# Newton's step of the norms in three instructions on VectorE, and two output transfers on ScalarE's queue

## The chip, the cores and the metric

The kernel runs on one core of a Trainium2 chip. The core has a matrix engine (TensorE, PE in the profile, with its weight loads as PEld), a vector engine (VectorE, DVE), a scalar engine (ScalarE, ACT), a general one (GpSimd, POOL) and SyncE (SP), which here only issues transfers. Each engine takes the instructions of its own queue in order. The metric is device time in microseconds (us); lower is better.

## The reference

Two layers of a hybrid block work on 512 latent tokens and 256 context tokens of width 1024. Layer 0 mixes by convolutions, layer 1 by windowed attention; each layer ends with a ConvFFN of inner width 2816, and the latents get a last RMSNorm. Every norm needs one inverse root per token:

```python
def rmsnorm(x, g):
    xf = x.astype(jnp.float32)
    y = xf * lax.rsqrt(jnp.mean(xf * xf, axis=-1, keepdims=True) + EPS)
    return (y * g.astype(jnp.float32)).astype(x.dtype)

x = x + g1 * y                                   # mixer of the layer
x = x + g2 * conv_ffn(modulate(rmsnorm(x, norm_ffn[l]), sh2, sc2), w_up[l], w_conv_ffn[l], w_down[l])
...
return rmsnorm(x, final_norm)
```

The layer norm in the convolution mixer uses the same inverse root.

## The kernel before

The activations lie transposed: 128 features on the partitions, tokens along the free axis, eight tiles `x[k]` of 128 features. A matrix product with a weight tile is made of three products of split operands (lines 185 to 187: low part of the weights, low part of the activations, both high parts). Weights come in by SyncE's queue (line 172), ScalarE casts the high part (line 166) and VectorE subtracts the low part (line 167).

A norm goes so. While the last product of a sub-layer is closed column by column (`project`, with `gate_in` at line 372 and `square_in` at lines 291 to 296), the squares are added up in `ss`. TensorE turns `ss` into one sum per token (line 303, the statistics), ScalarE adds the epsilon (line 306, tile `rv`), and `inverse` makes the inverse root `y`: a first guess on the bits (line 308) and three Newton steps of four instructions each (lines 310 to 313), on two, four or six numbers per partition. `rstd` spreads `y` on the diagonal of a tile `rd` (line 325, VectorE) and TensorE broadcasts it over the partitions (line 335); ScalarE copies the result to `r` (lines 444, 540, 646), and `mod_in` makes the next `h` from it (line 348 on VectorE, lines 357 to 362 on ScalarE and VectorE), which the next products read (lines 220 to 224, `side_by_side`).

`inverse` is used eleven times. The norm at the start and the two at the end pass VectorE as the engine. The other eight go through `rstd` with its default, GpSimd: two in the layer norm of the convolutions (`conv_norm`), and one for each of two token segments at the first ConvFFN, at the start of layer 1 and at the second ConvFFN (`spread`, called by `tokens_in_turn`). In `tokens_in_turn` the first segment's norm is made while TensorE still has columns of the second segment to do: `project` holds columns back (`late`), and lines 328 to 331 ask that two or three of them stand between the statistics and the broadcast.

The order in which the instructions of each engine stand in its queue is made when the kernel is built, by a planner that works with estimated durations (`schedule_with_timeline_sim=True`, line 1249). `issue_after` adds an edge to that order; it isn't a wait at run time.

At the end, `final` scales the transposed results by `y` into eight tiles `fo` of 128x512 and sends each out by a transfer of 256 KB (line 1156), all on SyncE's queue. The last four tiles (`both=True`) are made in turn by ScalarE (line 1154) and VectorE (line 1152).

Of the kernel before, what the change touches and what calls it, by code (L numbers as in the profile page):

```python
# [17 lines left out]
ALU = mybir.AluOpType  # L18
PSUM = bass.MemoryType.PSUM

P = 128
# [43 lines left out]
class Kern:  # L65
# [232 lines left out]
    def inverse(self, ss, chunks, ones2, comp, eng):  # L298

        nc = self.nc  # L300
        n = len(chunks)
        for i, c in enumerate(chunks):
            self.stats = nc.tensor.matmul(comp[:, 2 * i:2 * i + 2], ss[:, c:c + P], ones2, start=True, stop=True)
        v, y, t = (self.tmp.tile([P, 6], F32, name=g, tag=g)[:, :n] for g in ("rv", "ry", "rt"))
        means = comp[:, :2 * n].rearrange("p (n c) -> p n c", c=2)[:, :, 0:1].squeeze(2)
        self.means = nc.scalar.activation(v, means, AF.Copy, bias=EPS)

        eng.tensor_scalar(y.bitcast(I32), v.bitcast(I32), -0.5, float(0x5F3759DF), op0=ALU.mult, op1=ALU.add)
        for _ in range(3):
            eng.tensor_tensor(t, y, y, op=ALU.mult)  # L310
            eng.tensor_tensor(t, t, v, op=ALU.mult)
            eng.tensor_scalar(t, t, -0.5, 1.5, op0=ALU.mult, op1=ALU.add)
            eng.tensor_tensor(y, t, y, op=ALU.mult)
        return y

    def rstd(self, ss, segs, ones2, slot, eng=None, pool=None, project=None):

        nc = self.nc
        chunks = [c for lo, hi in segs for c in range(lo, hi, P)]
        n = len(chunks)  # L320
        o = slot
        off = segs[0][0] - segs[0][0] % C0
        y = self.inverse(ss, chunks, ones2, o[:, segs[0][0] - off:segs[0][0] - off + 2 * n], eng or nc.gpsimd)
        d = (pool or self.tmp).tile([P, n, P], F32, name="rd", tag="rd", bufs=1)
        nc.vector.tensor_tensor(
            d, self.ident.unsqueeze(1).broadcast_to([P, n, P]), y.unsqueeze(2).broadcast_to([P, n, P]), op=ALU.mult
        )
        if project:
            with self.tc.issue_after(self.stats.ins):
                next(project)  # L330
        i = 0
        with self.tc.issue_after(self.product.ins) if project else nullcontext():
            for lo, hi in segs:
                m = (hi - lo) // P
                nc.tensor.matmul(
                    o[:, lo - off:hi - off], self.onesm, d[:, i:i + m, :].rearrange("p n c -> p (n c)"), start=True, stop=True)
                i += m
        return o[:, segs[0][0] - off:segs[-1][1] - off]
# [805 lines left out]
    def final(self, seg, slots, y, both=True):  # L1144

        nc = self.nc
        for i, s in enumerate(slots):
            half, c = divmod(i, 2)
            tag, bufs = (("tC", 2), ("tC", 2), ("r", 1), ("rd", 1))[i] if both else (("tA", "tB")[c], 2)
            o = self.tmp.tile([P, 512], F32, name="fo", tag=tag, bufs=bufs)  # L1150
            if both and c:
                nc.vector.tensor_scalar(o, s, y[:, c:c + 1], None, op0=ALU.mult)
            else:
                nc.scalar.activation(o, s, AF.Copy, scale=y[:, c:c + 1])
            t = seg[0] + c * P
            nc.sync.dma_start(self.out[t:t + P, 512 * half:512 * half + 512], o)


def _rope_tables():
# [94 lines left out]
```

## Time and profile before

| what | value |
|---|---|
| median of 3 runs | 1461.03 us (1460.87 to 1461.33) |
| profiled execution, its own time | 1462.82 us |
| its span, first to last instruction | 1461.0 us |
| TensorE busy | 1421.9 us (97%) |
| VectorE busy | 1083.3 us (74%) |
| ScalarE busy | 649.8 us (44%) |
| GpSimd busy | 181.3 us (12%) |
| mean granted clock of TensorE | 0.997 |

The busy shares are means over stages with different limits. The rows below are of four kinds: totals of waits (who waited for whom, and how long), single instructions in order of time (start, duration, and in brackets the idle time before with what ended it), groups of one line's instructions with their durations, and stretches with each engine's busy time and the granted clock (1.00 is 2.4 GHz, 0.50 is 1.2 GHz).

### The profile page before, as it was taken

To read this page: it belongs to the slowest core of one execution; us is meant where nothing else is said; L and a number is where in the kernel's file an instruction comes from. 1 tells how busy PE (TensorE), PEld (TensorE's weight loads), DVE (VectorE), ACT (ScalarE), POOL (GpSimd) and SP (SyncE) were. 2 spreads that over 40 slices of the span, in tenths; PEclk is the share of its full clock that TensorE was granted. 3 is DMA by queue.
4 is the path that set the end of the run, shared out by engine and by line. 5 is a ranking of instruction groups with operands and counts; after the bars stand their busy time and mean duration, and the time that the engine had idled before them with its cause. 6 is when DMAs were issued, how large, how long until landed. Compare 5 with 4: busy or idle time off the path is not lost.

```text
span 1461.0 us, 24131 instructions
## 1 busy us (share of the span) xinstructions
PE 1421.9 (97%) x9470; PEld 1249.1 (85%) x9470; DVE 1083.3 (74%) x1750; ACT 649.8 (44%) x1105; POOL 181.3 (12%) x427
## 2 busy tenths in 40 slices
PE   5999999999999999999999999999999999999997
PEld 3888888888888888888888878867799999999897
DVE  6699998689878557565534679787767977777676
ACT  5422224473223223123213365687765745545455
POOL 0000001112222212112212110243200000000000
PEclk9999999999999999999999999999999999999999
DMA  9325433036787767847725315264532444444441
GB/s 375 113 71 174 159 116 130 30 101 204 212 223 190 218 194 197 250 156 185 162 98 100 111 59 159 67 134 110 122 116 97 157 152 158 146 156 157 148 130 68
DMA packets 80546, 215.69 MB, mean 148 GB/s; under 512 B 10032, under 2 KB 10160, under 8 KB 80304
## 3 DMA queue, kind: packets, MB, share of 16 engines
q1 hardware_dynamic: 63408, 174.29, 36.1%
q0 software_dynamic: 17024, 39.86, 13.0%
q8 instruction: 74, 1.21, 0.3%
q14 instruction: 40, 0.33, 0.1%
HBM read 209.39 MB, written 41.94 MB: 172 GB/s over the span
## 4 chain that ended last, share of the span: by engine, by line
PE 82%; DVE 7%; DMA 5%; ACT 3%; issue 2%; POOL 1%; SPq 0%; DVEq 0%; ACTq 0%
PE slot L185 20%; PE slot L186 20%; PE slot L187 19%; DMA wraw<-in_w_down 3%; PE av L1091 2%; DVE wlo L167 2%; PE pt L1081 2%; PE s L1062 2%; PE av L185 2%; PE av L186 2%; PE av L187 1%; ACT whi L166 1%; PE slot L220 1%; PE slot L224 1%; PE slot L221 1%
## 5 line engine op out<-in xcount | busy, mean ns | idle before, releaser
L185 PE MATMUL slot<-h,wlo 128*128 128x256 f32 (+1 forms) x1152 | 382.5, 334 | 2.8 <-DVE ub L582 1.2
L186 PE MATMUL slot<-h,whi 128*128 128x256 f32 (+1 forms) x1152 | 382.5, 333 | 0.2 <-DVE h L362 0.2
L187 PE MATMUL slot<-h,whi 128*128 128x256 f32 (+1 forms) x1152 | 382.7, 332 | 0.0
L166 ACT CAST whi<-wraw 128x1024 fp32r<-128x1024 f32 (+2 forms) x249 | 219.9, 892 | 240.8 <-PE slot L187 88.1
L167 DVE TENSOR_TENSOR wlo<-wraw,whi 128x1024 fp32r<-128x1024 f32 (+2 forms) x249 | 254.4, 1027 | 72.2 <-ACT whi L166 71.5
L185 PEld LDWEIGHTS slot<-h,wlo 128*128 128x128 f32 x1152 | 216.5, 188 | 29.0 <-issue 2.0
L186 PEld LDWEIGHTS slot<-h,whi 128*128 128x128 f32 x1152 | 217.0, 188 | 23.1 <-DVE h L362 0.5
L187 PEld LDWEIGHTS slot<-h,whi 128*128 128x128 f32 x1152 | 217.0, 188 | 21.8
L382 DVE SCALAR_TENSOR_TENSOR cf<-slot,par,cf 128x775 f32<-128x775 f32 (+1 forms) x92 | 92.6, 1009 | 97.8 <-ACT cf L380 97.7
L185 PE MATMUL slot<-gh,wlo 128*128 128x512 f32 (+1 forms) x435 | 148.8, 344 | 2.1 <-ACT gh L166 1.1
L186 PE MATMUL slot<-gl,whi 128*128 128x512 f32 (+1 forms) x435 | 147.9, 341 | 0.0
L187 PE MATMUL slot<-gh,whi 128*128 128x512 f32 (+1 forms) x435 | 147.6, 340 | 0.0
L380 ACT ACTIVATE cf<-slot,par 128x776 f32<-128x776 f32 (+1 forms) x46 | 41.4, 901 | 192.8 <-PE slot L187 188.7
L590 DVE SCALAR_TENSOR_TENSOR cacc<-ub,par,cacc 128x783 f32<-128x783 f32 x120 | 118.4, 1035 | 0.3
L266 DVE CUSTOM_DVE_ANT_0 junk<-wmod,cb 128x1024 bf16<-128x1024 f32 x80 | 97.5, 1218 | 22.1 <-DMA wmod<-in_wmt 20.5
L372 DVE SCALAR_TENSOR_TENSOR x<-slot,mod,x 128x256 f32<-128x256 f32 (+1 forms) x139 | 80.9, 612 | 40.9 <-PE slot L187 40.4
L185 PEld LDWEIGHTS slot<-gh,wlo 128*128 128x128 f32 x435 | 81.4, 188 | 12.7 <-ACT gh L166 1.3
L187 PEld LDWEIGHTS slot<-gh,whi 128*128 128x128 f32 x435 | 81.8, 188 | 9.8
L186 PEld LDWEIGHTS slot<-gl,whi 128*128 128x128 f32 x435 | 81.9, 188 | 9.6 <-DVE mod L247 0.2
L1069 DVE CUSTOM_DVE_ANT_0 sm<-s,mask,nsink 128x640 f32<-128x640 f32 (+1 forms) x58 | 46.6, 819 | 13.9 <-PE pt L1081 10.7
L860 ACT ACTIVATE sgf<-cf 128x776 f32<-128x776 f32 (+1 forms) x44 | 32.6, 742 | 53.6 <-DVE cf L382 53.6
L1072 ACT ACTIVATE sm<-sm,nm 128x513 f32<-128x513 f32 (+1 forms) x64 | 50.0, 785 | 10.7 <-DVE nm L1069 7.1
(333 smaller groups left out, 2873.3 us busy)
## 6 DMA issues: line engine op xcount, KB each, us to landing
s<-in_w_up POOLq DMA_DIRECT2D x114, 256.0 KB, 5.5
wmod<-in_wmt SPq DMA_DIRECT2D x56, 512.0 KB, 4.6
wraw<-in_w_up SPq DMA_DIRECT2D x50, 512.0 KB, 4.2
wmod<-in_wm SPq DMA_DIRECT2D x40, 512.0 KB, 5.1
wraw<-in_w_up SPq DMA_DIRECT2D x57, 256.0 KB, 2.9
wraw<-in_w_down SPq DMA_DIRECT2D x48, 256.0 KB, 3.1
wraw<-in_w_in SPq DMA_DIRECT2D x20, 512.0 KB, 3.9
wraw<-in_w_down SPq DMA_DIRECT2D x32, 320.0 KB, 3.0
```

The costliest lines, as they stand in the source:

```text
L166: self.act_mark = self.nc.scalar.copy(hi, src)
L167: self.mark = self.nc.vector.tensor_tensor(lo, src, hi.bitcast(F32), op=ALU.subtract)
L185: mm(out, lo, xh, start=first, stop=False)
L186: mm(out, hi, xl, start=False, stop=False)
L187: self.product = mm(out, hi, xh, start=False, stop=last)
L266: nc.vector.tensor_tensor_reduce(junk, w, self.cb[:, c, :], 1.0, 0.0, ALU.mult, ALU.add, col)
L372: self.nc.vector.scalar_tensor_tensor(self.x[k][:, lo:hi], acc, self.mod[:, l, chunk * 8 + k, c:c + 1], self.x[k][:, lo:hi], op0=ALU.mult, ...
L380: nc.scalar.activation(acc[:, :n], u[:, :n], AF.Copy, scale=w[:, 1:2])
L382: nc.vector.scalar_tensor_tensor(acc[:, o], u[:, i], w[:, j:j + 1], acc[:, o], op0=ALU.mult, op1=ALU.add)
L590: self.tapped = nc.vector.scalar_tensor_tensor(acc, ub[:, t:t + CB_N], w[:, t:t + 1], acc, op0=ALU.mult, op1=ALU.add)
L1069: scored = nc.vector.tensor_tensor_reduce(sm[:, :n], s[:, SEQ - nl:SEQ + CTX], mk, -SCALE, nsink[:, hd:hd + 1], ALU.add, ALU.min, nm)
L1072: self.scored = scored, nc.scalar.activation(sm[:, :n + 1], sm[:, :n + 1], AF.Exp, scale=-1.0, bias=nm, accum_out=z)
```

## The change

Newton's step y (1.5 - 0.5 v y y) is written with two fused instructions and one product, so a norm's chain has ten instructions in place of thirteen. The default engine of `rstd` becomes VectorE, so all eleven chains run there and none on GpSimd. And of the last four output transfers those of the two tiles that ScalarE makes are issued from ScalarE's queue, the other two from SyncE's.

```diff
         eng.tensor_scalar(y.bitcast(I32), v.bitcast(I32), -0.5, float(0x5F3759DF), op0=ALU.mult, op1=ALU.add)
         for _ in range(3):
-            eng.tensor_tensor(t, y, y, op=ALU.mult)
+            eng.scalar_tensor_tensor(t, y, -0.5, y, op0=ALU.mult, op1=ALU.mult)
             eng.tensor_tensor(t, t, v, op=ALU.mult)
-            eng.tensor_scalar(t, t, -0.5, 1.5, op0=ALU.mult, op1=ALU.add)
-            eng.tensor_tensor(y, t, y, op=ALU.mult)
+            eng.scalar_tensor_tensor(y, t, 1.5, y, op0=ALU.add, op1=ALU.mult)
         return y
...
-        y = self.inverse(ss, chunks, ones2, o[:, segs[0][0] - off:segs[0][0] - off + 2 * n], eng or nc.gpsimd)
+        y = self.inverse(ss, chunks, ones2, o[:, segs[0][0] - off:segs[0][0] - off + 2 * n], eng or nc.vector)
...
-            nc.sync.dma_start(self.out[t:t + P, 512 * half:512 * half + 512], o)
+            queue = nc.scalar if both and i % 2 == 0 else nc.sync
+            queue.dma_start(self.out[t:t + P, 512 * half:512 * half + 512], o)
```

## Rows read from the trace of the kernel before

**Rows 1.** The page's part 1: busy us, share of the span, instructions.
```profile
PE 1421.9 (97%) x9470; PEld 1249.1 (85%) x9470; DVE 1083.3 (74%) x1750; ACT 649.8 (44%) x1105; POOL 181.3 (12%) x427
```

**Rows 2.** Waits by pair: who waited for whom, us in total, times, longest.
```profile
DVE rd L325 <- POOL ry L313: 14.0, 6, 3.4
...
PE slot L634 <- ACT r L646: 0.5, 1, 0.5
```

**Rows 3.** One line's instructions: ns min/median/max, first and last start, forms.
```profile
L313 POOL TENSOR_TENSOR ry<-rt,ry x24: 194/196/575, 241.2 to 1108.5; 128x2 f32<-128x2 f32 x15, 128x4 f32<-128x4 f32 x9
...
L278 DVE SCALAR_TENSOR_TENSOR gain<-mod,par x7: 163/164/168, 26.1 to 624.2; 128x4 f32<-128x4 f32 x4, 128x16 f32<-128x16 f32 x2, 128x8 f32<-128x8 f32 x1
```

**Rows 4.** Timeline of layer 1's start: start, duration, engine, line, operation [idle before].
```profile
837.19 1.27 POOL L308 TENSOR_SCALAR ry<-rv 128x4 int32<-128x4 int32 x1 [30.78 <-ACT rv L306]
...
837.19 1.22 DVE L167 TENSOR_TENSOR wlo<-wraw,whi 128x1024 fp32r<-128x1024 f32 x1
...
842.15 0.69 DVE L325 TENSOR_TENSOR rd<-ident,ry 128x512 f32<-128x512 f32 x1 [1.29 <-POOL ry L313]
...
843.68 1.02 PE L335 MATMUL slot<-rd,onesm 128*128 128x512 f32 x2
...
845.35 0.57 ACT L540 COPY r<-slot 128x512 f32<-128x512 f32 x1
...
846.53 1.28 DVE L348 TENSOR_TENSOR xr<-x,r 128x512 f32<-128x512 f32 x2
...
846.66 0.61 PE L303 MATMUL slot<-ones,ss 128*128 128x2 f32 x4 [1.96 <-DVE ss L296]
...
847.38 1.51 ACT L357 ACTIVATE h<-xr,mod,gain 128x512 fp32r<-128x512 f32 x2
...
848.23 0.80 PE L220 MATMUL slot<-h,wlo 128*128 128x512 f32 x1 [0.96 <-ACT h L357]
```

**Rows 5.** Stretches: busy us of each engine (instructions), clock; the last two TensorE alone.
```profile
848.20:854.40 6.20, 6.17 (x15) 4.82 (x16) 3.35 (x7) 3.45 (x5) 4.92 (x12) 0.50 0.14 57
854.40:860.00 5.60, 5.60 (x26) 4.65 (x25) 5.33 (x10) 4.21 (x8) 0.00 (x0) 1.00 0.16 47
...
283.95:290.95 7.00, 7.00 (x61) 1.00 0.01 4
836.55:843.65 7.10, 7.10 (x62) 1.00 0.45 150
```

**Rows 6.** Timeline at the first ConvFFN's start.
```profile
288.36 0.69 DVE L325 TENSOR_TENSOR rd<-ident,ry 128x512 f32<-128x512 f32 x1 [0.78 <-POOL ry L313]
...
294.25 0.50 PE L220 MATMUL slot<-h,wlo 128*128 128x512 f32 x1 [0.73 <-ACT h L357]
```

**Rows 7.** Timeline of ScalarE behind the first norm of `conv_norm`.
```profile
248.90 0.62 ACT L166 CAST wo<-wraw 128x512 fp32r<-128x512 f32 x1 [4.49 <-DMA wraw<-in_w_out]
249.42 0.58 ACT L646 COPY r<-slot 128x512 f32<-128x512 f32 x1
```

**Rows 8.** Timeline of the tail, then stretches of it (last: clock, DMA share, GB/s).
```profile
1452.27 0.17 DVE L308 TENSOR_SCALAR ry<-rv 128x2 int32<-128x2 int32 x1 [0.96 <-ACT rv L306]
...
1454.65 0.16 DVE L313 TENSOR_TENSOR ry<-rt,ry 128x2 f32<-128x2 f32 x1
...
1455.62 0.33 SPq L1156 DMA_DIRECT2D out_x<-fo  x1
...
1457.05 0.39 SPq L1156 DMA_DIRECT2D out_x<-fo  x1
...
1453.75:1456.25 2.50, 0.03 (x1) 0.00 (x0) 2.19 (x8) 2.06 (x4) 0.00 (x0) 1.00 1.05 401
1456.25:1456.50 0.25, 0.00 (x0) 0.00 (x0) 0.11 (x1) 0.00 (x0) 0.00 (x0) 1.00 0.44 156
1456.50:1459.25 2.75, 0.00 (x0) 0.00 (x0) 0.00 (x0) 0.00 (x0) 0.00 (x0) 0.87 0.98 375
```

**Rows 9.** Timeline of VectorE behind the first norm.
```profile
20.71 3.49 DVE L167 TENSOR_TENSOR wlo<-wraw,whi 128x1024 fp32r<-128x1024 f32 x3
```

## The prediction

> **What bounds the kernel now.** I read the page's busy times first: TensorE is busy 97% of the span [rows 1]. A change that touches only VectorE, GpSimd and the output transfers can therefore gain in two places alone: where TensorE waits for a norm, and in the tail behind its last matmul. So next come the timelines around the eleven norms (line 306 to 313), the stretches' granted clock, and the tail. The waits by pair give one more figure: VectorE stood 14.0 us in six places before line 325, waiting for GpSimd's Newton chain [rows 2].
>
> The place that matters is the start of layer 1. TensorE finishes the held columns, makes the latent norm's broadcast (line 335) at 843.68, waits 1.96 us, makes the context statistics (line 303), waits 0.96 us more and only then has the first `h` (line 220 at 848.23) [rows 4]. Behind these two waits it runs at half clock (0.50, the lower of its two levels, 1.2 GHz): 15 matmuls in 6.20 us, 0.413 us each, against 26 in 5.60 us, 0.215 each, at the full clock after it [rows 5]. The place costs about 2.9 us of waiting and 15 x 0.2 = 3.0 us of clock. A shorter wait stands at the same point of the first ConvFFN (0.73 us [rows 6]).
>
> **The change part by part.**
>
> *Thirteen instructions become ten.* On VectorE one link of the chain takes 0.16 us, and the links start 0.2 us apart: twelve steps from 1452.27 to 1454.65, 0.198 us each [rows 8]. A scalar_tensor_tensor of this size has a row of its own, 0.164 us [rows 3], so nothing is paid for the fused form. The three chains that were on VectorE already drop three links, 0.6 us each.
>
> *Eight chains move from GpSimd.* There a link is 0.196 us in the median, up to 0.575 in this line alone [rows 3], and one in layer 1 took 1.27 us: it began at 837.19 together with VectorE's 1.22 us weight split and ended 0.05 us after it [rows 4]. I read this as GpSimd being held while VectorE makes the split. At that norm the chain began at 837.19 and line 325 at 842.15, so it took 4.96 us with its handover. On VectorE it takes 10 x 0.2 = 2.0 us alone and 1.22 more if the split goes first; two short pieces of 0.4 us may come between. So line 325 comes 0.9 us (4.0 us of chain) to 3.0 us earlier; I take 1.3, nearer to the loaded end, since the split is there in the rows. VectorE gets 8 x 2.0 = 16 us of added work and loses 14.0 us of waiting [rows 2]; it has room, so this is zero to first order, and its cover is VectorE's idle time. Gone, it would cost up to 2.0 us per norm.
>
> *What that is worth at layer 1.* The queues are filled in an order fixed when the kernel is built. Line 335 stands about 59 matmuls behind the statistics in the first ConvFFN and behind all 60 in layer 1 [rows 5], although line 325 was ready 0.8 us before that in layer 1 (842.15 + 0.69 = 842.84 against 843.68). The planner thus seems to allow some 7 us for the norm. A chain that is 1.3 us shorter in its estimate too moves line 335 by 1.3 / 0.115 = 11 matmuls, into the last column. From there the path is 1.02 us of line 335, 0.57 of the copy, 0.64 of one line 348 and 0.75 of one `h`: 3.0 us without queueing, where before it took 4.55 because the copy came at 845.35 and line 348 at 846.53 [rows 4]. Line 335 at 842.4 gives `h` at 845.4, while the columns behind it end at 844.7. Of the 2.92 us some 0.7 stay, 2.2 go, and with so short a wait I expect the full clock to hold: 3.0 more. The next thing late is `h` itself: the context norm's ten links (2.0 us) now stand among VectorE's work on `h`, and I give back 0.9 for that. Sum -4.3; the ends are 0 (the order stays) and -5.9 (all of it).
>
> *The first ConvFFN.* The wait is 0.73 us, and line 325 had stood 0.78 us for GpSimd [rows 6]. I take -0.6, between 0 and -0.73.
>
> *The conv norm.* Here the copy of `r` at 249.42 stands behind a cast that waited 4.49 us for a transfer of weights [rows 7]; a shorter chain helps only if the copy is put ahead of that cast. TensorE's wait that hangs on it is 0.5 us [rows 2]. I take -0.3, between 0 and -0.5.
>
> *The start.* The 0.6 us are hidden: behind the norm VectorE does three weight splits in 3.49 us [rows 9], and line 348, which needs `r`, stands behind them. I take 0, between 0 and -0.6. The other norms have no wait of TensorE behind them: 0.
>
> *The tail.* The last chain ends 0.6 us earlier, so the last four transfers could be issued 0.6 us earlier; and with ScalarE's queue for two of them SyncE no longer issues all four one after the other (1455.62 to 1457.05). But the sixteen DMA engines are already full: 1.05 of them from 1453.75 to 1456.25 and 0.98 from 1456.50 to 1459.25, with only a quarter microsecond at 0.44 between [rows 8]. Eight outputs of 256 KB have to drain at about 390 GB/s whoever issues them. What can be gained is the hole, 0.25 x 0.56 = 0.14 us, and a little of the 2%. I take -0.2, between -0.4 and +0.3. The upper end is for ScalarE's queue, which this trace never shows issuing a transfer: if ScalarE issues the first of its two before its second scaling (0.33 to 0.39 us by SyncE's rows [rows 8]), that scaling and the last issue are late by that much, most of it hidden by the same drain.
>
> By the Trainium skill (DMA: Bandwidth & Descriptors, section "Issuing engines are not separate DMA queues") transfers from all queues interleave on the same sixteen engines, and issuing from several saves only the time of issue. By that rule alone the second queue would save the two issues that it takes off SyncE, some 0.7 us, and the sum would be 0.5 us lower; the rows above say that the issue is not what the last landing waits for.
>
> **The sum.** -4.3 - 0.6 - 0.3 - 0.2 = -5.4 us. The profiled execution has a span of 1461.0 and took 1462.82 us, 1.8 us outside the span; the median of the runs is 1461.03. The terms are stretches of the span, so they come off either: 1461.03 - 5.4 = 1455.6 us.
>
> **The rivals.**
>
> *The order stays (0.32).* Line 335 remains behind all 60 columns in layer 1. For it: it waited there for no data (0.8 us of slack), so a chain that is earlier does nothing unless the planner's own estimate moves. Its estimate for GpSimd need not hold the stretched links that the trace shows, and then its gain is smaller than mine. What is left is the first ConvFFN, part of the conv norm and the tail: -0.6 - 0.2 - 0.2 = -1.0, 1460.0 us, from 1458.5 to 1461.5. The same result comes if the tail alone works.
>
> *Slower (0.15).* Before, the wait for `rv` was GpSimd's and cost nothing. On VectorE the first link (line 308) waits in a queue that runs in order, and everything behind it waits too. At layer 1 the context norm's chain is the one that can hurt: if it is put ahead of the first line 348, `h` comes 2.0 us later, TensorE's wait grows from 2.9 to 4.9, and the half clock lasts longer; half as long again is 1.5 us. With the other gains gone that is +3.5 to +5: 1465 us. It decides when line 308 stands before line 348 in VectorE's queue. Against it: line 348 is needed by work that is written earlier in the program.
>
> *The transfers don't move the end.* That is in my tail term already (0 in place of -0.2), and changes no sign.
>
> **How the numbers follow.** Forecast 0.53, order stays 0.32, slower 0.15. The likeliest is 1455.6 us. Its own range is 1452.9 (all ends taken: -5.9, -0.73, -0.5, start -0.6, tail -0.4, together -8.1) to 1458. The range of 8 in 10 takes in the case of the unchanged order and leaves out the slower one: 1452.9 to 1462.0. Faster by over 0.2% (2.9 us, about what a measurement of this kernel can tell from no change) has 0.53, within it 0.32, slower 0.15.
>
> **What would show it.** Right: line 335 of layer 1 with column matmuls behind it; no half clock near 848 us; line 325 with no wait for GpSimd anywhere; GpSimd without lines 308 to 313; links 0.2 us apart; the DMA engines full from 1453 on to within 0.3 us of the old length. Wrong: the two waits before line 220 still add to 2.9 us; a half-clock stretch at another norm; VectorE idle before line 308 with TensorE waiting for `h`; a last landing more than 0.5 us sooner behind the last line 303 than before, which would say that the issue, not the drain, set the tail.

## The result, and the profile after

The changed kernel takes 1473.40 us (median of 5 runs, 1471.71 to 1474.21), the kernel before 1461.06 us beside it: ratio 1.0081, 95% interval 1.0069 to 1.0092. It is 12.3 us slower, where 5.4 us less was predicted. The profiled execution has a span of 1471.4 us, 10.3 more than before. Three of the kernels below had one execution each that took far longer at a low clock (`queue_only` 2663 us, `conv_slow8` 2053, `conv_l1ctx_back` 7156); the ratios leave them out, and without them the medians of the first two would be 1461.05 and 1465.97 us.

First the engines, from the page of the changed kernel (busy us, share of the span, instructions), to be held against [rows 1]:

```profile
PE 1425.1 (97%) x9470; PEld 1251.4 (85%) x9470; DVE 1092.9 (74%) x1821; ACT 651.5 (44%) x1105; POOL 149.6 (10%) x323
```

The work moved as intended: GpSimd lost some 32 us, VectorE gained 10. To see where the time went, the span is cut at the starts of line 306 (`rv`), which each norm has once. Four stages matter: `conv_norm` (from its first norm to the latent norm of the first ConvFFN), the first ConvFFN (from there to layer 1's latent norm), layer 1's projections and attention (from its context norm to the next norm), and the second ConvFFN. Stretches of the kernel before, then of the changed one: start and end, length, busy us (instructions) of PE, PEld, DVE, ACT, POOL, then granted clock, DMA share, GB/s.

```profile
237.26:284.25 46.99, 45.31 (x233) 37.08 (x232) 34.08 (x62) 21.29 (x44) 7.75 (x26) 1.00 0.23 73
284.25:836.93 552.68, 551.20 (x3199) 485.95 (x3199) 366.40 (x518) 170.03 (x223) 110.66 (x213) 1.00 0.61 171
847.31:1073.74 226.43, 223.28 (x1482) 177.66 (x1483) 176.54 (x420) 157.90 (x339) 50.75 (x132) 0.98 0.42 103
1073.74:1444.92 371.18, 367.68 (x2694) 349.12 (x2694) 287.19 (x447) 210.33 (x367) 5.58 (x26) 1.00 0.44 139
```

```profile
236.97:291.10 54.13, 48.78 (x237) 39.75 (x236) 37.65 (x84) 21.52 (x44) 0.00 (x0) 0.94 0.20 64
291.10:845.60 554.50, 551.50 (x3199) 486.07 (x3199) 368.62 (x538) 170.00 (x224) 102.30 (x187) 1.00 0.61 170
855.89:1085.91 230.02, 222.96 (x1482) 176.64 (x1483) 177.57 (x430) 158.48 (x339) 44.70 (x119) 0.99 0.41 102
1085.91:1455.55 369.64, 366.50 (x2693) 348.59 (x2693) 290.78 (x467) 211.37 (x367) 0.00 (x0) 1.00 0.44 139
```

`conv_norm` is 7.1 us longer: TensorE's idle time in it (length minus PE busy) grew from 1.7 to 5.3, and its busy time by 3.5, with the same matmuls but a mean clock of 0.94. The first ConvFFN is 1.8 longer and layer 1's stage 3.6. The second ConvFFN is 1.5 us shorter, but that belongs to this one execution of the kernel before: in every other profile shown here the stage takes 368.3 to 370.7 us. So the loss is 7.1 + 1.8 + 3.6 = 12.5, less 0.3 at the end: 12.2 us, where the medians say 12.3.

**Where `conv_norm` loses it.** VectorE's timeline in the changed kernel: start, duration, engine, line, operation, in brackets the wait before it. Line 308 to 312 is the chain of the first norm, all on 128x4 numbers; `rv` was ready at 237.14, and the chain starts 3.1 us later, behind gates and two large splits.

```profile
240.26 0.17 DVE L308 TENSOR_SCALAR ry<-rv 128x4 int32<-128x4 int32 x1
240.34 0.69 DVE L167 TENSOR_TENSOR wo<-wraw,wo 128x512 fp32r<-128x512 f32 x1
240.94 1.14 DVE L371 SCALAR_TENSOR_TENSOR x<-slot,mod,x 128x512 f32<-128x512 f32 x2
241.99 0.15 DVE L310 SCALAR_TENSOR_TENSOR rt<-ry 128x4 f32<-128x4 f32 x1
242.40 0.69 DVE L167 TENSOR_TENSOR wo<-wraw,wo 128x512 fp32r<-128x512 f32 x1 [0.26 <-ACT wo L166]
243.01 0.15 DVE L311 TENSOR_TENSOR rt<-rt,rv 128x4 f32<-128x4 f32 x1
243.20 0.16 DVE L312 SCALAR_TENSOR_TENSOR ry<-rt,ry 128x4 f32<-128x4 f32 x1
244.37 0.69 DVE L167 TENSOR_TENSOR wo<-wraw,wo 128x512 fp32r<-128x512 f32 x1 [1.01 <-ACT wo L166]
...
249.22 0.16 DVE L312 SCALAR_TENSOR_TENSOR ry<-rt,ry 128x4 f32<-128x4 f32 x1
249.41 0.69 DVE L324 TENSOR_TENSOR rd<-ident,ry 128x512 f32<-128x512 f32 x1
```

A link takes the 0.16 us that was forecast, but the next link does not follow it. Seven of the nine gaps hold weight splits or gates, and three of the splits wait for their cast (0.26, 1.01 and, not shown, 0.80 us). Ten links that need 2 us take 9.1 from the start of the first to the end of the last; thirteen on GpSimd took 6.1 and started at once. Line 324 comes 12.3 us after `rv` was ready; in the kernel before, where it is line 325, that is 6.2 us:

```profile
243.66 0.69 DVE L325 TENSOR_TENSOR rd<-ident,ry 128x512 f32<-128x512 f32 x1 [3.44 <-POOL ry L313]
```

TensorE in the changed kernel, and last the same stretch of time in the kernel before:

```profile
252.30 1.02 PE L334 MATMUL slot<-rd,onesm 128*128 128x512 f32 x2
...
257.69 1.52 PE L185 MATMUL slot<-gh,wo 128*128 128x512 f32 x3 [2.12 <-ACT gh L166]
259.96 0.80 PE L186 MATMUL slot<-gl,wo 128*128 128x512 f32 x1 [0.75 <-DVE gl L167]
...
257.85:264.68 6.83, 6.08 (x14) 4.30 (x15) 5.14 (x10) 4.09 (x9) 0.00 (x0) 0.50 0.22 74
...
257.85:264.68 6.83, 6.67 (x30) 4.88 (x28) 4.29 (x10) 1.59 (x5) 2.30 (x12) 1.00 0.39 131
```

The broadcast (line 334, line 335 before) does not even wait for its data. It stands 92 matmuls of the columns behind the norm's statistics, before 50; so the columns are used up when it comes, and behind it TensorE waits 2.12 and 0.75 us for what hangs on `r`. A third new wait, 1.42 us at 280.48, ends with a small VectorE instruction (line 106) that stands behind work on `r` as well. From 257.85 to 264.68 the granted clock is 0.50, its lower level; the kernel before has 1.00 there.

**Where layer 1 loses it.** VectorE at layer 1's start in the changed kernel, the chain of the context norm:

```profile
856.85 0.16 DVE L308 TENSOR_SCALAR ry<-rv 128x2 int32<-128x2 int32 x1
856.92 0.54 DVE L357 TENSOR_SCALAR ht<-xr,gain,mod 128x512 f32<-128x512 f32 x1
...
858.58 0.15 DVE L310 SCALAR_TENSOR_TENSOR rt<-ry 128x2 f32<-128x2 f32 x1
...
864.56 0.15 DVE L312 SCALAR_TENSOR_TENSOR ry<-rt,ry 128x2 f32<-128x2 f32 x1
```

One or more pieces of `h` follow every link, so the chain takes 7.9 us (6.5 on GpSimd), and the broadcast starts 12.6 us after `rv` was ready, before 7.8. The broadcast doesn't wait for its data here either. TensorE's queue is laid out for a late one. Before, 36 matmuls of the first two query products stood behind the last one of the keys (870.89 to 879.07 us) and ran while the keys were copied for the rotation. Now the queue has most of them ahead, as work to be done until the context part of `h` is there, and seven are left for the copies. TensorE in the kernel before, then in the changed one:

```profile
855.31 0.59 PE L335 MATMUL slot<-rd,onesm 128*128 128x256 f32 x2
...
870.89 0.39 PE L185 MATMUL slot<-h,wlo 128*128 128x512 f32 x1
...
878.84 0.39 PE L187 MATMUL slot<-h,wq 128*128 128x512 f32 x1
```

```profile
868.69 0.60 PE L334 MATMUL slot<-rd,onesm 128*128 128x256 f32 x2
...
884.81 0.39 PE L187 MATMUL slot<-h,wq 128*128 128x512 f32 x1
888.83 0.50 PE L185 MATMUL slot<-h,wlo 128*128 128x512 f32 x1 [3.64 <-ACT rp L918]
```

**Where the first ConvFFN loses it.** Its context broadcast starts 10.5 us after `rv` was ready (before 7.8), twelve matmuls of the product that follows (lines 185 to 187) are put ahead of the context columns, and at 337.55 line 185 waits 1.64 us, where before it did not wait. But the chain isn't late here. It takes 4.3 us and starts 0.75 us after `rv`, on GpSimd it took 5.6; `rd` is made 5.1 us after `rv`, 0.6 us sooner than before, and is then left lying for 5.0 us. VectorE and TensorE in the kernel before (`rv` ready at 299.91), then in the changed one (306.72):

```profile
305.66 0.42 DVE L325 TENSOR_TENSOR rd<-ident,ry 128x256 f32<-128x256 f32 x1 [2.29 <-POOL ry L313]
307.75 0.60 PE L335 MATMUL slot<-rd,onesm 128*128 128x256 f32 x2
```

```profile
311.85 0.43 DVE L324 TENSOR_TENSOR rd<-ident,ry 128x256 f32<-128x256 f32 x1
317.27 0.60 PE L334 MATMUL slot<-rd,onesm 128*128 128x256 f32 x2
...
337.55 0.47 PE L185 MATMUL slot<-h,wlo 128*128 128x512 f32 x1 [1.64 <-ACT whi L166]
```

So what this stage loses follows the order of TensorE's queue, which is made at build from estimated durations, and not a chain that ends late.

### The profile page after: what moved, and what is told of

Read it like the earlier page. It is cut to its first block, busy times and chain, and to the rows that moved or that the text cites. A ratio compares the mean times of both kernels' runs of the same rounds, so it can differ in the third digit from the quotient of the medians.

```text
span 1471.4 us, 24094 instructions
## 1 busy us (share of the span) xinstructions
PE 1425.1 (97%) x9470; PEld 1251.4 (85%) x9470; DVE 1092.9 (74%) x1821; ACT 651.5 (44%) x1105; POOL 149.6 (10%) x323
## 4 chain that ended last, share of the span: by engine, by line
PE 87%; DVE 5%; DMA 3%; ACT 3%; issue 2%; SPq 1%; POOL 0%; DVEq 0%; ACTq 0%; POOLq 0%
PE slot L185 21%; PE slot L186 21%; PE slot L187 21%; PE av L1090 2%; DMA wraw<-in_w_down 2%; PE pt L1080 2%; PE s L1061 2%; PE av L185 2%; PE av L186 2%; PE av L187 2%; PE pt L185 1%; PE pt L187 1%; PE pt L186 1%; PE slot L238 1%; DVE wlo L167 1%
## 5 line engine op out<-in xcount | busy, mean ns | idle before, releaser
L166 ACT CAST whi<-wraw 128x1024 fp32r<-128x1024 f32 (+2 forms) x249 | 220.1, 892 | 235.5 <-PE slot L187 90.2
L700 POOL COPY tk<-cf 128x1 f32<-128x1 f32 x41 | 18.4, 450 | 406.4 <-DVE cf L381 379.3
```

The source lines that it names most:

```text
L166: self.act_mark = self.nc.scalar.copy(hi, src)
```

## The experiments

Two theories stood at first. **A**: a chain that stands in VectorE's in-order queue gets other work between its links, its `r` comes late, and TensorE's queue is laid out anew around the later broadcast. **B**: the fused form, or the order that it brings, makes the loss. The stages of each kernel are read as above (from its own line 306), the last stage from the last `rv` to the end of the span:

| kernel | us | ratio, 95% interval | `conv_norm` (clock) | first ConvFFN | layer 1 | end |
|---|---|---|---|---|---|---|
| before | 1461.06 | | 46.99 (1.00) | 552.68 | 226.43 | 8.97 |
| changed | 1473.40 | 1.0069 to 1.0092 | 54.13 (0.94) | 554.50 | 230.02 | 8.64 |
| vector_four | 1474.47 | 1.0073 to 1.0106 | 50.63 (1.00) | 555.33 | 232.18 | 8.96 |
| fused_where_vector | 1461.87 | 0.9987 to 1.0006 | 46.99 (1.00) | 552.66 | 226.36 | 8.80 |
| queue_only | 1461.28 | 0.9987 to 1.0006 | 46.87 (1.00) | 552.76 | 226.38 | 8.90 |
| conv_back | 1466.98 | 1.0020 to 1.0046 | 46.99 (1.00) | 554.42 | 231.47 | 8.74 |
| conv_l1ctx_back | 1462.54 | 1.0003 to 1.0022 | 46.98 (1.00) | 554.45 | 227.16 | 8.73 |
| ctx_conv_back | 1460.93 | 0.9991 to 1.0010 | 46.79 (1.00) | 552.62 | 226.45 | 8.74 |
| conv_only | 1468.92 | 1.0041 to 1.0071 | 53.51 (0.97) | 552.77 | 228.74 | 8.68 |
| conv_tight | 1472.49 | 1.0066 to 1.0096 | 55.93 (0.94) | 553.68 | 231.12 | 8.66 |
| two_steps | 1465.78 | 1.0019 to 1.0043 | 49.87 (1.00) | 552.92 | 227.05 | 8.70 |
| conv_slow8 | 1466.76 | 1.0026 to 1.0053 | 52.25 (1.00) | 552.70 | 226.27 | 8.86 |
| l1ctx_slow8 | 1466.26 | 1.0021 to 1.0047 | 47.07 (1.00) | 552.64 | 231.73 | 8.91 |
| early_stats | 1461.40 | 0.9991 to 1.0010 | 47.37 (1.00) | 551.56 | 223.78 | 8.86 |

Where a stage has the chains and the queue of before, its lengths agree within 0.3 us (early_stats apart, which changes layer 1's start), so a difference of 1 us in these stages is taken as real, though each length is from one execution. A ratio is against runs of the kernel before made beside it.

### The parts alone

`vector_four` is the kernel before with this:

```diff
-        y = self.inverse(..., eng or nc.gpsimd)
+        y = self.inverse(..., eng or nc.vector)
```

> The eight chains on VectorE, with the old thirteen instructions and with all outputs on SyncE's queue: the move alone. Theory A (other work gets between the links of a chain that stands on VectorE, and TensorE's queue is laid out anew around the later broadcast): the whole loss is here, and three more links per chain make it no smaller: 1472 to 1478 us against 1461, conv_norm's first chain 9 us or longer, a half-clock stretch near 258 us. Theory B (the fused form, or the order that it brings, is the loss): 1461 +- 1.5 us.

1474.47 us: the move alone makes the whole loss. Its first chain in `conv_norm` takes 9.7 us. There is no half clock in that stage of the profiled execution, unlike what A said, and the stage is 3.5 us shorter than in the changed kernel, while the first ConvFFN and layer 1 are together 3.0 us longer. That execution is the quickest of four (1472.72 us, with a mean clock of 0.997 over the span); the other three have 0.993 to 0.994 and take 1474.31 to 1476.27 us, so the half clock can differ from one execution to the next, and where they had it isn't recorded.

`fused_where_vector` takes the fused loop only where the engine is VectorE (the thirteen-instruction loop stays for GpSimd), and no chain moves:

```diff
+            if eng is nc.gpsimd:
+                ...
+            else:
+                eng.scalar_tensor_tensor(t, y, -0.5, y, op0=ALU.mult, op1=ALU.mult)
+                eng.tensor_tensor(t, t, v, op=ALU.mult)
+                eng.scalar_tensor_tensor(y, t, 1.5, y, op0=ALU.add, op1=ALU.mult)
```

> The fused ten instructions only in the three chains that stood on VectorE before (first norm, the two final norms); the other eight stay on GpSimd with thirteen; outputs as before. Theory A: no chain moves, so 1461 +- 1.2 us: the start costs +0.7 as in the changed kernel (if that was the fused form's doing) and the tail gains up to 0.6. Theory B: most of the loss is here, 1467 us or more.

1461.87 us, no difference. Theory B falls. `queue_only` has the diff's last hunk alone:

```diff
-            nc.sync.dma_start(self.out[...], o)
+            queue = nc.scalar if both and i % 2 == 0 else nc.sync
+            queue.dma_start(self.out[...], o)
```

> Only the output queue changed: two of the last four output transfers from ScalarE's queue. Theories A and B: the end moves by -0.4 to +0.3 us, 1460.7 to 1461.4 us, since the sixteen DMA engines are full up to the end. Theory C (the second queue itself costs the end): 1462 us or more.

1461.28 us, no difference: theory C falls too.

### Chains put back on GpSimd

In the changed kernel, with the fused loop kept on VectorE:

```diff
-            nc.scalar.copy(rs[i], self.rstd(ss, [(0, n)], self.ones2b, at))
+            nc.scalar.copy(rs[i], self.rstd(ss, [(0, n)], self.ones2b, at, eng=nc.gpsimd))
```

> The changed kernel with the two chains of conv_norm back on GpSimd (thirteen instructions there); everything else as changed. Theory A: the drift of 6.3 us between 237 and 283 us goes, and no half clock near 258 us; the waits near 336 and 885 us stay: 1467.0 us (1466 to 1468.5). Theory B: 1473 us still.

1466.98 us, as A has it: `conv_norm` is back at 46.99, the other two stages stay long. `conv_l1ctx_back` puts layer 1's context chain back as well, `ctx_conv_back` the context chains of both ConvFFNs too (`eng=self.nc.gpsimd` in `spread` for the second segment).

> The changed kernel with conv_norm's chains and layer 1's context chain on GpSimd; both chains of the two ConvFFNs and layer 1's latent chain on VectorE. Theory A: against the kernel with conv_norm's alone put back (1467.0), the wait of 4.0 us at the first line 185 after the rope copies goes and the 1.8 us near 330 us stays: 1463 us (1462 to 1464.5). Rival D: 1466 to 1467 us.

> The changed kernel with conv_norm's two chains and the three context chains (first ConvFFN, layer 1's start, second ConvFFN) back on GpSimd; the three latent chains stay on VectorE. Theory A: the waits near 336 us (1.8) and at the first line 185 after the rope copies (4.0) come from the context chains that stretch on VectorE, so both go: 1461.5 us (1460 to 1463), as before. Rival D (any chain on VectorE brings them, the latent ones too): 1466 to 1467 us, as with conv_norm's two alone put back.

1462.54 and 1460.93 us. Layer 1's stage falls from 231.47 to 227.16 with its own context chain, the first ConvFFN from 554.45 to 552.62 with its own, each chain moving its own stage by 1.8 to 4.3 us and no other by more than 0.7. What is left in `ctx_conv_back` (three latent chains on VectorE, the fused form, the second queue) is worth nothing that can be measured. The reverse, the kernel before with `conv_norm`'s chains alone on VectorE (`eng=nc.vector` at the same line; the fused loop in every chain on VectorE, which `fused_where_vector` found to cost nothing):

> The kernel before with conv_norm's two chains alone on VectorE (and the fused form in every chain on VectorE). Theory A: this is the other half of what putting them back took away: +6 us, 1467 us (1466 to 1468.5), first chain near 9 us, half clock near 258 us. Rival H (conv_norm costs this much only beside the other moves): 1463 us or less.

1468.92 us, a little above what A allowed, so rival H falls. `conv_norm` gives 6.5 of the 8.0 us. Layer 1's stage is also 2.3 longer, though none of its chains is changed; TensorE's queue there is in another order than before, and it waits 1.51 and 0.89 us in places where before it did not. Why a change in `conv_norm` reorders that stage, and not in `conv_slow8`, is open.

### What about the chain costs

Two readings of A were left. **L**: it is enough that `r` comes late, whichever engine makes it late. **V**: the links harm by standing ahead of splits and gates that TensorE needs. `conv_slow8` and `l1ctx_slow8` leave the chains on GpSimd and lengthen them, by the same argument in `conv_norm` (shown) and in `spread` for layer 1's context:

```diff
-        for _ in range(3):
+        for _ in range(steps):
-            nc.scalar.copy(rs[i], self.rstd(ss, [(0, n)], self.ones2b, at))
+            nc.scalar.copy(rs[i], self.rstd(ss, [(0, n)], self.ones2b, at, steps=8))
```

> The kernel before with eight Newton steps in place of three in conv_norm's two chains, still on GpSimd (the extra steps don't change what is computed), so that r comes about as late as in the changed kernel (first chain 11 to 14 us in place of 6.1; 9.1 on VectorE), while VectorE's queue holds no link. Theory L (what costs is that r comes late, whichever engine makes it so): 1465 to 1468 us, with TensorE's waits and half clock near 255 us. Theory V (what costs is that the links stand in VectorE's own queue, ahead of splits and gates that TensorE needs): 1463 us or less.

> The kernel before with eight Newton steps in place of three in layer 1's context chain alone, on GpSimd. Theory L: its line 335 is queued some 25 matmuls later, work that covered the rope copies is put ahead of it, and the first line 185 after those copies waits 2 to 4 us: 1463 to 1465.5 us. Theory V: no wait there, 1461 to 1462 us.

1466.76 and 1466.26 us, as L has it: lateness is enough to cost this much, with no link on VectorE. TensorE in `l1ctx_slow8`, then VectorE and TensorE in `conv_slow8`:

```profile
857.58 0.39 PE L224 MATMUL slot<-h,whi 128*128 128x512 f32 x1
863.17 1.22 PE L335 MATMUL slot<-rd,onesm 128*128 128x256 f32 x2 [5.21 <-DVE rd L325]
```

```profile
249.60 0.69 DVE L325 TENSOR_TENSOR rd<-ident,ry 128x512 f32<-128x512 f32 x1 [3.22 <-POOL ry L313]
...
250.44 1.10 PE L335 MATMUL slot<-rd,onesm 128*128 128x512 f32 x2 [1.16 <-DVE rd L325]
```

In `conv_slow8`, `rd` comes 13.1 us after `rv` was ready (12.3 in the changed kernel), and the stage is 5.3 us longer at full clock. The changed kernel's 7.1 us is of that order, plus the half clock, which costs at most half of 6.83 us; a clean split of it this is not, since `conv_slow8` also makes the stage's second chain 10.0 us long (5.5 in the changed kernel, 3.6 before) and waits at both broadcasts themselves. In one point L was wrong: in `l1ctx_slow8` the loss is not at the rotation but at the broadcast itself, which waits 5.21 us for a chain that took 15.7 us, longer than I had reckoned. That covering work moved ahead brings the wait behind the keys is thus read from the two orders; `l1ctx_slow8` shows only what lateness costs. No run keeps TensorE's order of before with the chains on VectorE, so lateness and order aren't priced apart. At the places of before (7.1, 7.8 and 7.8 us after `rv`) the broadcast would have to wait in `conv_norm` and at layer 1, where `rd` is finished 13.0 and 9.6 us after `rv`, and not in the first ConvFFN (5.5).

`conv_tight` takes V's side. In the changed kernel, the weight splits of columns 3 to 7 are written behind the chain:

```diff
-        with self.tc.issue_after(self.tapped.ins):
-            first += [self.weights(w[m][:, half], 4 * P, place(m)) for m in range(3, KT)]
         ...
         self.conv_norm(slots[0], y)
+        with self.tc.issue_after(self.newton.ins):
+            first += [self.weights(w[m][:, half], 4 * P, place(m)) for m in range(3, KT)]
```

> The changed kernel, but the weight splits of the output projection's columns 3 to 7 are queued on VectorE behind the last link of conv_norm's first chain. All chains stay on VectorE. Theory A (the splits between the links make the chain 9.1 us): the chain takes 4 us or less, line 334 comes as early as before, no half clock near 258 us, most of the 6.3 us goes: 1468 us (1466.5 to 1470). Rival E (VectorE is simply full there; what is taken from between the links is missing behind them): 1472 us or more.

1472.49 us: rival E, nothing gained. VectorE, then TensorE:

```profile
235.09 0.16 DVE L308 TENSOR_SCALAR ry<-rv 128x4 int32<-128x4 int32 x1
235.28 0.16 DVE L310 SCALAR_TENSOR_TENSOR rt<-ry 128x4 f32<-128x4 f32 x1
...
236.85 0.16 DVE L312 SCALAR_TENSOR_TENSOR ry<-rt,ry 128x4 f32<-128x4 f32 x1
236.93 1.89 DVE L167 TENSOR_TENSOR wo<-wraw,wo 128x512 fp32r<-128x512 f32 x3
...
237.67 0.80 PE L185 MATMUL slot<-gh,wo 128*128 128x512 f32 x1 [3.50 <-DVE wo L167]
```

The chain is as fast as the prediction had it, ten links in 1.92 us, 0.196 from start to start; so the fused links cost nothing by themselves. But now TensorE waits 3.50 us for the first split behind them, and the granted clock falls here too (a mean of 0.94). In this place VectorE's queue has no room: what goes from between the links is missing behind them. The edit also moves loads (the next three of `w_up` are issued from 238.9 us on, not from 225.4), so the size of this loss is no clean price.

`two_steps` makes the chains of the changed kernel shorter instead, by leaving out one Newton step of three:

```diff
-        for _ in range(3):
+        for _ in range(2):
```

> The changed kernel with two Newton steps in place of three in every chain (part of the computation is left out), so seven links in place of ten. Theory A (each link on VectorE costs its place between other pieces): conv_norm's first chain falls from 9.1 to some 6.5 us and the layer-1 context chain from 7.9 to some 5.5; the time falls by a quarter to a half of the loss: 1469 us (1467 to 1471.5). Rival F (the number of links doesn't matter, the loss is made by the wait for the first one and by the order): 1472.5 to 1474 us.

1465.78 us, well below what A gave and further from rival F. In `conv_norm` the first chain falls from 9.1 to 6.8 us, at layer 1 from 7.9 to 5.9: the three links that went are worth 2.0 to 2.3 us, 0.7 each and not 0.2, which fits a piece of other work for each. All three stages shrink, and in this execution `conv_norm` has no half clock, which is part of its 4.3 us.

### What the largest term was worth

`early_stats` is the kernel before with layer 1's latent norm begun one held column earlier:

```diff
-        project = self.project(wd, len(last) * P, last, segs, l, 5, lead=2, late=6, few=(2, 4), room=room)
+        project = self.project(wd, len(last) * P, last, segs, l, 5, lead=2, late=6, few=(1, 4), room=room)
```

> The kernel before, with nothing changed but that layer 1's latent norm begins one held column earlier. It measures what the two waits and the half clock at layer 1's start are worth, the largest term of the prediction. As the prediction has it: line 335 comes 1.5 us earlier, the first wait (1.96 us) goes, no half clock follows: 4.3 us less than before, 1457.5 us (1455.9 to 1459). Rival G (the waits stay or move, since the context statistics and h are late too): 1460.5 to 1462 us.

1461.40 us, rival G. Layer 1's start in it, TensorE's timeline and a stretch:

```profile
844.39 1.02 PE L335 MATMUL slot<-rd,onesm 128*128 128x512 f32 x2
...
847.96 0.50 PE L220 MATMUL slot<-h,wlo 128*128 128x512 f32 x1 [1.85 <-ACT h L357]
...
850.19 1.01 PE L303 MATMUL slot<-ones,ss 128*128 128x2 f32 x4 [0.79 <-DVE ss L296]
...
849.96:856.78 6.82, 6.59 (x18) 5.34 (x19) 4.46 (x9) 4.24 (x7) 4.54 (x10) 0.50 0.22 77
```

Line 335 does have column matmuls behind it, six of them where the prediction reckoned with eleven. The columns end at 846.1, `h` comes 1.85 us later, the context statistics wait 0.79 on top, and the half clock follows as before. The two waits are 2.64 us in place of 2.92, and from the first ConvFFN's latent norm to the norm behind layer 1's attention it is 790.1 us, before 789.5.

## Why the prediction was wrong, point by point

**What bounds the kernel** was right: TensorE is busy 97% of the span in both, and the loss is TensorE's idle time and its clock behind norms.

**Thirteen instructions become ten: right.** Links on VectorE are 0.196 us apart when nothing stands between (0.2 forecast), and the fused form has no price.

**Eight chains move: this step failed.** It had line 325 come 1.3 us sooner at layer 1, counted 2.0 us of links for every norm, and called VectorE's 16 us "zero to first order", since they took the place of 14.0 us of waiting [rows 2]. The sum was made in busy time; the cost is in order. At layer 1's latent norm, the place it was made for, the chain takes 4.4 us with 1.22 before it, so `rd` comes 5.6 us after `rv` in place of 5.1, later and not sooner. In `conv_norm` it is 9.1 + 3.1, and at the context norms 4.3 and 7.9, beside 6.1, 5.6 and 6.5 on GpSimd. Where VectorE has nothing else to do the chain does gain: 1.9 us in place of 3.5 and 4.1 in the second ConvFFN, where TensorE waits for nothing. The 14.0 us were no room. VectorE waited there at line 325 because its queue had got that far; the new links stand earlier, among splits, gates and pieces of `h`. The prediction did say that the cover is VectorE's idle time and that it costs up to 2.0 us per norm when gone; it didn't ask, norm by norm, what stands in VectorE's queue between `rv` and `rd`, nor where TensorE's queue would put the broadcast and the work that covers it: in the first ConvFFN that alone cost 1.8 us, with `rd` sooner than before.

The Trainium skill (Perfetto Trace Analysis, section "Optimizing GPSIMD Operations") says: "Prefer implementations on other engines where possible." A chain of small instructions is an exception that this case shows: a link starts 0.28 us after the one before it on GpSimd and 0.196 on VectorE when nothing comes between, but in `conv_norm` and at layer 1's context the chain as a whole was quicker in GpSimd's own queue.

**Layer 1's start, -4.3: not there, and mis-sized.** The order stayed, as the first rival had it: line 334 still stands behind all columns, and the waits are 1.87 and 0.96 us in place of 1.96 and 0.96 [rows 4]. The prediction moved the broadcast by eleven matmuls because the chain gets shorter. But it stands 60 matmuls behind the statistics with thirteen links on GpSimd (before), thirteen on VectorE (`vector_four`), ten (changed) and seven (`two_steps`): its place here does not follow the length of the chain. `early_stats` shows that a broadcast six matmuls earlier in the columns brings nothing (what eleven would bring no run shows): the path from it to `h` took 3.6 us in place of the 3.0 reckoned without queueing, and the context statistics follow with a wait of their own. The half clock did not come at this place in the changed kernel (below), though the waits stayed.

**First ConvFFN, -0.6:** the wait before its first line 220 went from 0.73 to 0.63 us. The stage lost 1.8 by its context norm, to which the prediction gave 0 ("the other norms have no wait of TensorE behind them"). That reckoning failed at this norm, at layer 1's context norm (0.9 us given back, for `h`) and in `conv_norm`: these norms had no wait, or a short one, because work covered them, and it was the cover that was laid out anew.

**`conv_norm`, -0.3 (0 to -0.5): +7.1.** The bounds were made from TensorE's wait before, 0.5 us [rows 2], and from a chain that could only get shorter. No end on the side of a loss was set, though the splits there wait for casts, and these for transfers [rows 7].

**The start, 0: right**; from the first norm to `conv_norm`'s first the changed kernel takes 220.1 us, the kernel before 220.3.

**The tail, -0.2: right.** The last chain takes 1.93 us in place of 2.54, and from the last `rv` to the end it is 8.64 in place of 8.97. Stretches of the changed kernel's tail, to be held against [rows 8]:

```profile
1466.65:1466.90 0.25, 0.00 (x0) 0.00 (x0) 0.25 (x2) 0.00 (x0) 0.00 (x0) 1.00 1.03 401
1466.90:1469.65 2.75, 0.00 (x0) 0.00 (x0) 0.61 (x1) 0.00 (x0) 0.00 (x0) 0.99 1.01 383
```

The quarter microsecond at 0.44 is now at 1.03: the hole is filled and the rest drains at the same rate. The table's last column splits it: 8.90 with the second queue alone, 8.80 and 8.68 (conv_only) with the fused form alone, 8.64 to 8.74 with both, 8.86 to 8.97 with neither. So the gain, some 0.2 us, is the shorter chain's. That agrees with the view taken from the rows, and not with the 0.7 us that the prediction names beside it for two issues saved.

**The rivals.** "The order stays" described layer 1's start rightly and still gave 1460.0, since it kept the gains elsewhere. "Slower" had the right sign and named layer 1's context norm, one of the three places; but its mechanism (line 308 ahead of the first line 348, `h` 2.0 us late) did not occur: line 308 stands at 856.85, behind the first two pieces at 855.11 and 855.71, and `h` was not delayed. The price came later, through `r`.

## What to carry to other kernels

Before a chain of dependent small instructions is moved to an engine, look at what stands in that engine's queue between the chain's input and its use: in an order fixed at build, each link can cost a whole piece of other work (here 0.7 us in place of 0.2), and a free share of the engine (26% here) didn't show it. Look also at where the waiting engine's queue puts the result's use, since that can move for the worse though the chain gets quicker. A slower engine with an empty queue can be the better place. And a norm that TensorE doesn't wait for isn't free: ask how late its result may come before the work that covers it, and the work that this cover was to hide later, is used up.

## What the runs showed of the hardware

The granted clock did not follow the waits in the way that the prediction took for granted. At layer 1's start the changed kernel has the same two waits as before, and then this, where the kernel before ran at 0.50 [rows 5]; behind the wait of 3.64 us the clock did fall:

```profile
856.80:863.00 6.20, 6.18 (x26) 4.91 (x27) 6.20 (x18) 4.88 (x8) 0.00 (x0) 1.00 0.15 61
889.40:892.60 3.20, 3.20 (x9) 2.45 (x8) 3.11 (x7) 2.31 (x6) 0.00 (x0) 0.50 0.69 219
```

The same holds between kernels: `conv_norm` with late chains ran at a mean of 0.94, 0.97 and 1.00. The mean of 0.94 over 54.1 us (6.83 of them at 0.50) is worth up to 3.4 us, that of 0.97 over 53.5 us about half as much. It holds within a kernel too: the mean over the span is 0.993 to 0.997 in the four executions of `vector_four`, and 0.995 to 0.999 in twenty of the kernel before. So much can come or go beside the waits, and a term for the clock needs both ends. Which kernel of the table has a half clock in which stage is thus known for one execution each.

Single links on GpSimd stretched much further than the 1.27 us that the prediction names: the longest took 2.79 us in the kernel before, one of 128x2 numbers 4.60 us in `l1ctx_slow8` and one of 128x4 2.92 us in `conv_slow8`, beside 0.19 to 0.20 for most.

```profile
847.85 4.60 POOL L311 TENSOR_TENSOR rt<-rt,rv 128x2 f32<-128x2 f32 x1
237.44 2.92 POOL L312 TENSOR_SCALAR rt<-rt 128x4 f32<-128x4 f32 x1
```

VectorE ran without a gap in both stretches, nearly all of it pieces that read two tiles. The Trainium skill (SBUF — State Buffer, section "SBUF: two separate sides") says that the two engines share a port pair which one of them holds for a whole instruction while the other waits; among others this concerns a VectorE instruction with two inputs in SBUF beside a GpSimd one that reads SBUF. The trace agrees with that so far as the long links lie in such stretches; no run here tests it.
